# RMSNorm sums from a second, token-major load of x, taken on ScalarE, in a hybrid decoder block

## The chip, the core and the metric

The kernel runs on one core of one Trainium2 chip, alone. The metric is the device time of one execution, in microseconds (us); the time before is the median of three runs, 1137.67 us (1136.68 to 1137.91).

A core has engines that run side by side, each through a queue of its own in order: TensorE (PE; its weight loads are listed apart as PEld), VectorE (DVE), ScalarE (ACT), GpSimd (POOL) and SyncE (SP), which here only issues DMAs. Matmuls write to banks of PSUM, which DVE and ACT read; the other tiles are in SBUF.

## The reference

One decoder block over 1024 tokens of width 1024, in float32:

```python
h = _rmsnorm(x, g_mix_pre)                       # x * rsqrt(mean(x*x, -1) + 1e-6) * g
proj = h @ w_in + b_in
u_pool, q, k, v, gates = split(proj)             # widths 512, 512, 128, 128, 2048
y_pool = multiscale_pool(u_pool, w_pool, pool_scale)
q, k = partial_rotary(q), partial_rotary(k)      # 8 query heads, 2 key/value heads of 64
y_attn = sliding_window_sink_attention(q, k, v)  # blocks of 128 tokens, window 128
g_pool, g_attn = split(sigmoid(gates))
mix = (g_pool * (y_pool @ w_branch_pool) + g_attn * (y_attn @ w_branch_attn)) @ w_out
x = x + _rmsnorm(mix, g_mix_post)
h2 = _rmsnorm(x, g_mlp_pre)
x = x + _rmsnorm(square(relu(h2 @ w_up)) @ w_down, g_mlp_post)
```

The change concerns only the first line, the sum of x*x for each token, and the order of work up to the end of attention.

## The kernel before

Tokens are taken in 8 blocks of 128 (index n), the width in 8 slices of 128 (index k). Each float32 operand is split into a high and a low part (`split`: ACT makes the high part at L101, DVE the low part at L104), and each product is three matmuls, high x high, low x high and high x low (`PASSES`).

**The load stage** (L205 to L242) runs over k. `xt[k]` is x with the width on the partitions and the 1024 tokens along the free axis. Each step loads `xt[k]` (512 KB) and the weights `w_qkv[k]` (384 KB), on SP's queue. ACT writes the high part of x times the norm's gain (L227), DVE the low part (L228), in two halves of 512 tokens; both split the weights. Then PE adds slice k to the queries (`mm_q`, L183) and to the keys and values (`mm_kv`, L192) of blocks 0 to 3, which stay open in PSUM over all k. The row factor r1 of the norm is not needed for this: it is applied later.

For r1, ACT squares `xt[k]` (L233, L235, in place), and POOL (for the last k, DVE) adds the squares up in `sq` (L236). The load of a later step into the same tile waits for that add. The tile tags bound how far loads run ahead: x tiles have 4 buffers (`s4`), staged weights 3 (`st`). The order of instructions in this stage is set by the scheduler of the framework, from the program order and the dependencies.

**The start of attention** (from L722) is ordered by hand for PE, DVE and ACT. `sq` is still a sum with the width on the partitions, so eight products with a column of ones (L725, 16 instructions on PE, `ones` is a column of `vec`) give the token sums in PSUM (`bss`). `rsqrt` turns them into r1 (L109 on ACT, then a chain on DVE). `pre_qkv(n)` scales the queries, keys and values of a block by r1, adds the bias (L264, L265, on DVE, which frees their PSUM banks) and applies the rotary embedding (L272 to L275, on DVE for block 0, on POOL for the others). `post_qkv(n)` transposes queries and keys on PE (L294, L295), splits them (ACT and DVE) and copies the values (POOL). `score` (L333), `softmax_*`, `attend_t` (L376) and `attend_v` (L394) follow.

**The filler.** All other products of this phase come from a generator, `others()`: queries, then keys and values of blocks 4 to 7, then the pooling branch's products. `fill(t)` takes steps from it until t microseconds of an assumed cost are spent (a query step of three matmuls counts 0.681, a key/value step 0.36); what is spent too much is owed by the next `fill`. So `fill` says how much of that work PE does at each place in the order. Its PSUM banks carry the tag `mm` (3 buffers): the queries of blocks 2 and 3 hold two of them until `pre_qkv(2)` and `pre_qkv(3)` have read them. `load_u(g)` stages weights of the pooling branch, and a list `between` holds the split of them until `flush` puts it in the order.

Everything behind attention (gates, output, MLP in seven products of halves) is left as it is.

Of the kernel before, what the change touches and what calls it, by code (L numbers as in the profile page):

```python
# [8 lines left out]
F32 = mybir.dt.float32  # L9
F32R = mybir.dt.float32r  # L10
AF = mybir.ActivationFunctionType
ALU = mybir.AluOpType
AX = mybir.AxisListType

P = 128
S = 1024
D = 1024
NT = S // P
NK = D // P
# [23 lines left out]
V_BU = V_G + 8  # L43
V_BG = V_BU + 4
V_PS = V_BG + 16
V_ONE = V_PS + 4
V_N = V_ONE + 1


@with_exitstack  # L50
def block_kernel(ctx: ExitStack, tc, xt, x, consts, vecs, sinks, b_qkv, g_post, g_mlp, g_mlp_post,
                 w_qkv, w_u, w_g, w_pool, w_bp, w_ba, w_o, w_up, w_dn, x1_dram, spill, wbp_dram, f_dram, out):
    nc = tc.nc
# [30 lines left out]
    def at(tag, bufs, shape, dt=F32):  # L84
        return ap_.tile([P] + shape, dt, tag=tag, name=nm(tag), bufs=bufs)

    def bank(tag, shape=None):
        return psum["pool"].tile([P] + (shape or [512]), F32, tag=tag, name=nm(tag), bufs=psum["bufs"][tag])
# [100 lines left out]
    def mm_kv(n, k, joint=False):  # L189

        for j, (xh, h) in enumerate(PASSES):
            pe.matmul(bkv_of(n), xs_[k][n // 4][:, xh, n % 4 * P:(n % 4 + 1) * P],  # L192
                      wkv[k // 2][:, h, k % 2, :], start=k == 0 and j == 0 and not (joint and n % 2),
                      stop=k == NK - 1 and j == 2 and not (joint and n % 2 == 0))
# [1 line left out]
    bq01 = bank("sc", [2, 512])  # L196
    bq = {0: bq01[:, 0, :], 1: bq01[:, 1, :], 2: bank("mm"), 3: bank("mm")}
    bkv = {0: bank("at", [2, 256]), 2: bank("at", [2, 256])}
    bss = bank("at", [NT])
    bz = bank("mm")  # L200
    for j in range(11):
        pe.matmul(bz, zeros[:, 0, :P], zeros[:, 0, :], start=j == 0, stop=j == 10)
    sq = at("qkv", 3, [S])
    ones = vec[:, V_ONE:V_ONE + 1]
    for k in range(NK):  # L205
        xs = at("s4", 4, [S])
        ws = stage([768]) if k else ws_first
        if k < 2:
            nc.sync.dma_start(xs[:, :512], xt[k][:, :512])
            if k:  # L210
                nc.sync.dma_start(ws, w_qkv[k])
            else:
                nc.sync.dma_start(vec, vecs)
                nc.sync.dma_start(ws[:, 512:], w_qkv[k][:, 512:])
            nc.sync.dma_start(xs[:, 512:], xt[k][:, 512:])
        else:
            nc.sync.dma_start(xs, xt[k])
            nc.sync.dma_start(ws, w_qkv[k])
        halves_ = [xp.tile([P, 2, 512], F32R, tag="x", name=nm("x")) for _ in range(2)]
        gk = vec[:, V_G + k:V_G + k + 1]  # L220
        q = wslot([2, 512]) if k < 6 else ga_.tile([P, 2, 512], F32R, tag="ga", name=nm("wq"))
        if k % 2 == 0:
            wkv.append(ga_.tile([P, 2, 2, 256], F32R, tag="ga", name=nm("wkv")))
        kv = wkv[-1]
        for th, t in enumerate(halves_):
            c = slice(th * 512, (th + 1) * 512)
            act.activation(t[:, 0, :], xs[:, c], AF.Identity, scale=gk)  # L227
            dve.scalar_tensor_tensor(t[:, 1, :], xs[:, c], gk, f32(t[:, 0, :]), ALU.mult, ALU.subtract)  # L228
            if th == 0:
                split(q[:, 0, :], q[:, 1, :], ws[:, :512])  # L230
                split(kv[:, 0, k % 2, :], kv[:, 1, k % 2, :], ws[:, 512:])
        if k == 0:
            act.activation(sq, xs, AF.Square)  # L233
        else:
            act.activation(xs, xs, AF.Square)  # L235
            (pool if k < NK - 1 else dve).tensor_tensor(sq, sq, xs, ALU.add)  # L236
        xs_.append(halves_)
        wq.append(q)
        for n in range(4):
            mm_q(n, k, bq[n])  # L240
        for n in range(4):
            mm_kv(n, k, joint=True)  # L242
    nc.sync.dma_start(cst, consts)
    nc.sync.dma_start(snk, sinks.unsqueeze(0).broadcast_to([P, NH]))
    bq_b = bcast(b_qkv, 768)
# [291 lines left out]
    def flush(todo):  # L537
        while todo:
            todo.pop(0)()
# [66 lines left out]
    def others():  # L606
        for n in range(4, NT):
            flush(late)
            bq[n] = bank("mm")
            for k in range(NK):  # L610
                mm_q(n, k, bq[n])
                yield 3 * 0.227
            if n == NT - 1:
                load_u(3)
                flush(between[1])
            bkv[n] = bank("at" if n == 4 else "mm", [1, 256])
            for k in range(NK):
                mm_kv(n, k)
                yield 3 * 0.12
            if n == 4:  # L620
                late.append(lambda: pre_qkv(4))
            else:
                pre_qkv(n)
        wps = stage([4, P])
        nc.sync.dma_start(wps, w_pool)
        between[0].append(lambda: split(wpt[:, 0], wpt[:, 1], wps))
        wpt = bcp.tile([P, 2, 4, P], F32R, tag="bc", name="wpt")
        wpts.append(wpt)
        for gi in (3, 2, 1, 0):
            load_wb(gi)  # L630
            if gi:
                load_u(gi - 1)
            yield from u_half(gi, 0)
            if gi < 3:
                yield from wb_half(gi + 1, 1)
            yield from u_half(gi, 1)
            yield from wb_half(gi, 0)
        yield from wb_half(0, 1)
# [81 lines left out]

    LOW, HIGH = range(4), range(4, 8)
    with tc.manual_schedule(engines={mybir.EngineType.PE, mybir.EngineType.DVE, mybir.EngineType.Activation}):  # L722
        for n in range(NT):
            fill(0.34)
            pe.matmul(bss[:, n:n + 1], sq[:, n * P:(n + 1) * P], ones, start=n == 0, stop=n == NT - 1)  # L725
        rsqrt(r1, bss[:, :NT], NT)
        act.activation(warm, r1[:, :1], AF.Exp)
        pre_qkv(0)
        pre_qkv(1)
        fill(5.4)  # L730
        post_qkv(0)
        pre_qkv(2)
        fill(2.8)
        score(0, 0)
        score_prev(0, 0)
        pre_qkv(3)
        fill(1.0)
        score(0, 1)
        score_prev(0, 1)
        fill(0.7)  # L740
        post_qkv(1)
        softmax_max(0)
        make_rb(0)
        fill(0.7)
        make_rb(1)
        softmax_exp(0, range(3))
        fill(1.8)
        score(1, 0)
        score_prev(1, 0)
        softmax_exp(0, range(3, 8))  # L750
        post_qkv(2)
        fill(0.7)
        score(1, 1)
        softmax_scale(0)
        score_prev(1, 1)
        softmax_max(1)
        fill(3.7)
        sums = {}

        def pump(k, gi):  # L760

            if gi not in sums:
                sums[gi] = pool_in(gi, us[gi], y_place)
            for _ in range(k):
                next(sums[gi])

        for n in range(NT):
            attend_t(n)
            if n == 0:
                softmax_exp(1, LOW)  # L770
            if n + 2 < NT:
                score(n + 2, 0)
            if n + 1 < NT:
                softmax_exp(n + 1, HIGH)
            if n + 2 < NT:
                score_prev(n + 2, 0)
            attend_own(n)
            if n + 1 < NT:
                softmax_scale(n + 1)
            flush(late)  # L780
            if n in (4, 5):
                pump(1, 3)
            elif n == 6:
                pump(1, 2)
            fill(3.6)
            if n + 2 < NT:
                score(n + 2, 1)
                score_prev(n + 2, 1)
                softmax_max(n + 2)
            if n + 3 < NT:  # L790
                post_qkv(n + 3)
            if n + 2 < NT:
                softmax_exp(n + 2, LOW)
            if n == 4:
                pump(1, 3)
            elif n == 5:
                pump(2, 3)
                nc.sync.dma_start(u_dram[3], us.pop(3))
            elif n == 6:
                pump(2, 2)  # L800
                load_x(0, lambda: at("qkv", 3, [S]))
            elif n == 7:
                pump(1, 2)
                nc.sync.dma_start(u_dram[2], us.pop(2))
                gt.prepare(0)
            fill(3.0 if n == NT - 1 else 4.2)
            attend_v(n)
            if n % 4 == 3:
                for kh in range(2):
                    nc.sync.dma_start(y_dram[n // 4 * 2 + kh], flat(y[n // 4][kh]))  # L810
        gt.prepare(1)
        fill(1e3)
        flush(between[0])
        flush(between[1])
        gt.prepare(2)
        load_x(1, lambda: ga_.tile([P, S], F32, tag="ga", name=nm("xr")))
        for _ in build_gate(0, lambda: xp.tile([P, 2, 512], F32R, tag="x", name=nm("T"))):
            pass
# [565 lines left out]
def _layout(inputs):  # L1384
    a = {k: np.asarray(v) for k, v in inputs.items()}
    f = np.float32
# [16 lines left out]
    for col, t in ((C_COS, np.cos(ang)), (C_SIN, np.sin(ang))):  # L1403
# [4 lines left out]
        b_in[:512].reshape(4, P).T,  # L1408
        b_in[1280:].reshape(16, P).T,
        a["pool_scale"][0].reshape(4, P).T,  # L1410
        np.ones((P, 1), f),
    ], axis=1)
    return [
        ("xt", c(x.T).reshape(NK, P, S)),
# [38 lines left out]
```

## Time and profile before

| | |
|---|---|
| runs | 1136.68, 1137.67, 1137.91 us; median 1137.67 |
| span of the profiled execution, first to last instruction | 1136.2 us |
| median less that span | 1.5 us |
| PE busy | 1120.7 us, 99% of the span |
| DVE, ACT, POOL busy | 822.7, 523.9, 65.3 us |
| mean granted clock of TensorE | 0.996 |
| DMA | 186.94 MB, mean 165 GB/s |

The profile is of one execution. Its own time is the span, with whatever lies before the first and behind the last instruction, which the profile does not show. A busy PE is not PE at its peak: a lower granted clock makes the same matmul longer and still busy.

### The profile page before, as it was taken

The page shows a single profiled execution, that of the slowest core. Times are in us where ns is not written, and L with a number is a line of the kernel's source. Part 1 is how long each engine was busy: PE and PEld are TensorE (multiplying, and loading weights), DVE is VectorE, ACT ScalarE, POOL GpSimd, SP SyncE. Part 2 cuts the span into 40 slices and gives each one's busy share as a digit, 9 for nine tenths or more (in the row PEclk, how much of TensorE's full clock was granted, in tenths as well). Part 3 has the DMA queues.
Part 4 walks back from the last instruction along what each step waited for, and adds up shares of the span by engine and source line. Part 5 has one row for each costly group of instructions (what it writes and reads, how often), then busy time and mean ns, then how long its engine had stood idle before and what let it go on. Part 6 is the DMA issues. An engine that isn't in the chain of part 4 may idle for free.

```text
span 1136.2 us, 14006 instructions
## 1 busy us (share of the span) xinstructions
PE 1120.7 (99%) x5213; PEld 926.6 (82%) x5213; DVE 822.7 (72%) x1210; ACT 523.9 (46%) x912; POOL 65.3 (6%) x110
## 2 busy tenths in 40 slices
PE   8999999999999999999999999999999999999997
PEld 7888888888888888888788888888888888888885
DVE  7668797899956685677998666666457955446887
ACT  6346655454522234455655444444444345344352
POOL 3432100000000230000000000000000000000000
PEclk9999999999999999999999999999999999999999
DMA  7202338356664434333265343434687765332652
GB/s 247 84 1 74 116 108 297 129 188 229 217 234 161 139 142 155 112 145 111 108 236 206 139 164 142 160 146 156 223 321 278 244 198 193 109 93 74 219 191 91
DMA packets 72052, 186.94 MB, mean 165 GB/s; under 512 B 6448, under 2 KB 10672, under 8 KB 71984
## 3 DMA queue, kind: packets, MB, share of 16 engines
q1 hardware_dynamic: 66368, 166.38, 42.0%
q10 hardware_dynamic: 5616, 19.66, 4.5%
q8 instruction: 41, 0.67, 0.2%
q14 instruction: 27, 0.22, 0.1%
HBM read 132.54 MB, written 53.48 MB: 164 GB/s over the span
## 4 chain that ended last, share of the span: by engine, by line
PE 91%; DVE 5%; ACT 2%; DMA 2%; issue 1%; DVEq 0%
PE mm L485 22%; PE at L485 15%; PE at L1291 14%; PE mm L1291 11%; PE mm L1008 6%; PE mm L422 5%; PE mm L575 4%; PE mm L183 3%; PE mm L424 3%; PE at L394 2%; PE sc L333 1%; PE at L1008 1%; PE at L192 1%; DVE wh L104 1%; DMA st<-in_w_up_dram 1%
## 5 line engine op out<-in xcount | busy, mean ns | idle before, releaser
L1291 PE MATMUL at<-ar,wh 128*128 128x512 f32 x744 | 169.6, 389 | 0.0
L1291 PEld LDWEIGHTS at<-ar,wh 128*128 128x128 f32 x744 | 139.6, 188 | 29.3 <-DVE ar L104 0.4
L1291 PE MATMUL mm<-ar,wh 128*128 128x512 f32 x576 | 131.0, 389 | 0.0
L104 DVE TENSOR_TENSOR wh<-raw,wh 128x1024 fp32r<-128x1024 f32 x53 | 64.8, 1223 | 85.4 <-ACT wh L101 85.4
L1291 PEld LDWEIGHTS mm<-ar,wh 128*128 128x128 f32 x576 | 108.1, 188 | 22.5
L101 ACT CAST wh<-raw 128x1024 fp32r<-128x1024 f32 x53 | 55.8, 1053 | 135.8 <-PE at L1291 61.9
L101 ACT CAST wh<-st 128x512 fp32r<-128x512 f32 (+1 forms) x105 | 66.2, 642 | 104.0 <-PE at L485 31.0
L104 DVE TENSOR_TENSOR wh<-st,wh 128x512 fp32r<-128x512 f32 (+1 forms) x105 | 81.8, 790 | 25.9 <-ACT wh L101 23.3
L485 PE MATMUL mm<-gr,wh 128*128 128x512 f32 x309 | 74.5, 390 | 0.1
L485 PEld LDWEIGHTS mm<-gr,wh 128*128 128x128 f32 x309 | 57.7, 188 | 12.3 <-ACT g L1073 0.5
L485 PE MATMUL mm<-T,wx 128*128 128x512 f32 x288 | 67.6, 389 | 0.0
L485 PEld LDWEIGHTS mm<-T,wx 128*128 128x128 f32 x288 | 54.1, 188 | 11.2
L485 PE MATMUL at<-T,wx 128*128 128x512 f32 x252 | 59.1, 389 | 0.0
L485 PEld LDWEIGHTS at<-T,wx 128*128 128x128 f32 x252 | 47.3, 188 | 9.8
L485 PE MATMUL mm<-x,wh 128*128 128x512 f32 x240 | 55.2, 389 | 0.0
L485 PEld LDWEIGHTS mm<-x,wh 128*128 128x128 f32 x240 | 45.0, 188 | 9.4
L104 DVE TENSOR_TENSOR ar<-B,ar 128x1024 fp32r<-128x1024 f32 x37 | 45.1, 1219 | 5.3 <-ACT ar L101 5.0
L575 PE MATMUL mm<-x,wh 128*128 128x512 f32 x192 | 47.5, 396 | 0.0
L485 PE MATMUL at<-gr,wh 128*128 128x512 f32 x174 | 42.4, 390 | 0.0
L101 ACT CAST ar<-B 128x1024 fp32r<-128x1024 f32 x37 | 38.9, 1050 | 7.5 <-DMA B<-in_w_dn_dram 4.7
L575 PEld LDWEIGHTS mm<-x,wh 128*128 128x128 f32 x192 | 35.2, 188 | 7.7
L485 PEld LDWEIGHTS at<-gr,wh 128*128 128x128 f32 x174 | 32.6, 188 | 7.3 <-DVE gr L104 0.5
(368 smaller groups left out, 2182.9 us busy)
## 6 DMA issues: line engine op xcount, KB each, us to landing
raw<-f_dram SPq DMA_DIRECT2D x53, 512.0 KB, 3.7
f_dram<-g SPq DMA_DIRECT2D x30, 512.0 KB, 3.3
B<-in_w_dn_dram SPq DMA_DIRECT2D x24, 512.0 KB, 6.2
st<-in_w_up_dram SPq DMA_DIRECT2D x22, 512.0 KB, 3.5
st<-in_w_g_dram SPq DMA_DIRECT2D x18, 512.0 KB, 3.6
f_dram<-g ACTq DMA_DIRECT2D x17, 512.0 KB, 2.6
g<-spill_dram SPq DMA_DIRECT2D x16, 512.0 KB, 4.5
raw<-in_w_dn_dram SPq DMA_DIRECT2D x16, 512.0 KB, 4.6
```

The lines of the kernel that those rows point to most:

```text
L101: act.copy(hi, src)
L104: eng.tensor_tensor(lo, src, f32(hi), ALU.subtract)
L183: pe.matmul(bq, xs_[k][n // 4][:, xh, n % 4 * P:(n % 4 + 1) * P], wq[k][:, h, :], start=k == 0 and j == 0, stop=k == NK - 1 and j == 2)
L192: pe.matmul(bkv_of(n), xs_[k][n // 4][:, xh, n % 4 * P:(n % 4 + 1) * P], wkv[k // 2][:, h, k % 2, :], start=k == 0 and j == 0 and not (joi ...
L333: pe.matmul(sb[:, kv, i, :nk], qt[r, qx, m * P:(m + 1) * P], kx[r, k0:k0 + nk], start=j == 0, stop=j == 2)
L394: pe.matmul(yb.rearrange("p m q -> p (m q)"), v[:, vh, kv * HD:kv * HD + P], p[ph][:, 4 * kv:4 * kv + 4].rearrange("p i q -> p (i q)"), st ...
L422: pe.matmul(bs[th], whi[:, k, :], rhs(k, hl, th), start=k == 0 and hl == 0, stop=False)
L424: pe.matmul(bs[th], wlo[:, k, :], rhs(k, 0, th), start=False, stop=k == nk - 1)
L485: pe.matmul(b, w[:, wh, kt, :], xo[kt][:, xh, :], start=not after and kt == 0 and j == 0, stop=kt == 3 and j == 2, skip_group_check=after)
L575: pe.matmul(b, (whi, wlo)[h][:, k, :], xr(k, xh, th), start=j == 0, stop=j == len(mms) - 1)
L1008: pe.matmul(obs[n][dj], l, wos[k][whl][:, dj * 512:(dj + 1) * 512], start=k == 0 and hl == 0 and whl == 0, stop=k == NK - 1 and hl == 1)
L1291: pe.matmul(bs[t], fo[fh][:, k2, t * P:(t + 1) * P], wo_[wh][:, k2, :], start=not after and s2 == 0 and k2 == 0 and j == 0, stop=s2 == NS ...
```

## The change

- The eight squares of `xt[k]`, the seven adds and the 16 instructions of L725 go, with `bss`, `sq` and the column of ones.
- x is loaded a second time, with tokens on the partitions: eight loads of `x[n]` (512 KB each), each squared on ACT with the sum over the free axis written to `ssq[:, n]`. The loads of `token_square(n)` take tiles of the tag `s8` (3 buffers), which the scores use later. `token_square(0)` stands in the step k = 2, and so on; 6 and 7 behind the loop.
- `rsqrt` reads `ssq` directly.
- In the order by hand, the eight `fill(0.34)` between the products go, `pre_qkv(2)` stands ahead of `post_qkv(0)`, and `fill(5.4)` becomes `fill(7.0)`.
- In `others()`, `load_u(3)` and the `flush` of `between[1]` come earlier: the load after the queries of block 6, the flush in the middle of those of block 7.

The short description of the change also says that keys of the second half are made ahead of queries; in the diff, `mm_kv(n)` follows `mm_q(n)` in `others()` as before.

```diff
@@ load stage
-    bss = bank("at", [NT])
...
-    sq = at("qkv", 3, [S])
-    ones = vec[:, V_ONE:V_ONE + 1]
+    ssq = sp.tile([P, NT], F32, name="ssq", bufs=1)
+
+    def token_square(n):
+
+        t = at("s8", 3, [D])
+        nc.sync.dma_start(t, x[n])
+        act.activation(t, t, AF.Square, accum_out=ssq[:, n:n + 1])
+
     for k in range(NK):
...
-        if k == 0:
-            act.activation(sq, xs, AF.Square)
-        else:
-            act.activation(xs, xs, AF.Square)
-            (pool if k < NK - 1 else dve).tensor_tensor(sq, sq, xs, ALU.add)
+        if k >= 2:
+            token_square(k - 2)
...
         for n in range(4):
             mm_kv(n, k, joint=True)
+    for n in (6, 7):
+        token_square(n)
     nc.sync.dma_start(cst, consts)
@@ others()
             for k in range(NK):
                 mm_q(n, k, bq[n])
+                if n == NT - 1 and k == 3:
+                    flush(between[1])
                 yield 3 * 0.227
-            if n == NT - 1:
+            if n == NT - 2:
                 load_u(3)
-                flush(between[1])
@@ order by hand
-        for n in range(NT):
-            fill(0.34)
-            pe.matmul(bss[:, n:n + 1], sq[:, n * P:(n + 1) * P], ones, start=n == 0, stop=n == NT - 1)
-        rsqrt(r1, bss[:, :NT], NT)
+        rsqrt(r1, ssq, NT)
         act.activation(warm, r1[:, :1], AF.Exp)
         pre_qkv(0)
         pre_qkv(1)
-        fill(5.4)
+        pre_qkv(2)
+        fill(7.0)
         post_qkv(0)
-        pre_qkv(2)
         fill(2.8)
         score(0, 0)
```

More of the change, by code (lines that the diff above doesn't have):

```diff
@@ L45 @@
 V_PS = V_BG + 16
-V_ONE = V_PS + 4
-V_N = V_ONE + 1
+V_N = V_PS + 4
 @with_exitstack
@@ L1410, in _layout @@
         a["pool_scale"][0].reshape(4, P).T,
-        np.ones((P, 1), f),
     ], axis=1)
```

## The prediction

> **What bounds the kernel now.** I read the page first, for the share of each engine; then the busy time by stretches of time; then the timeline and the chain of waits for the first 62 us, the only part that the change touches.
>
> ```profile
> span 1136.2 us, 14006 instructions
> PE 1120.7 (99%) x5213; PEld 926.6 (82%) x5213; DVE 822.7 (72%) x1210; ACT 523.9 (46%) x912; POOL 65.3 (6%) x110
> ```
>
> TensorE (PE) is busy 99% of the span, so time is gained only where PE idles, runs at a low clock, or does work that can go. All of it ahead of the attention loop is in the stretches below: start:end, length, then busy time and (instructions) of PE, PEld, DVE, ACT and POOL, the granted clock, the DMA share and GB/s.
>
> ```profile
> 0.00:8.00 8.00, 6.38 (x19) 4.52 (x20) 2.88 (x7) 4.34 (x7) 1.25 (x11) 1.00 0.72 212
> 8.00:14.00 6.00, 6.00 (x36) 5.31 (x35) 3.98 (x7) 5.33 (x10) 1.05 (x1) 1.00 1.03 408
> 14.00:24.00 10.00, 8.45 (x46) 6.90 (x45) 9.69 (x8) 7.55 (x13) 6.48 (x3) 1.00 0.54 191
> 24.00:30.00 6.00, 6.00 (x39) 5.42 (x38) 5.84 (x8) 3.11 (x5) 2.41 (x1) 1.00 0.74 239
> 33.45:37.63 4.18, 4.18 (x26) 3.69 (x25) 4.05 (x6) 2.22 (x4) 1.94 (x2) 1.00 0.27 65
> 52.85:55.52 2.67, 0.00 (x0) 0.00 (x0) 1.69 (x4) 0.85 (x2) 2.17 (x7) 1.00 0.00 0
> 55.52:60.12 4.60, 4.60 (x14) 3.37 (x14) 1.39 (x3) 0.00 (x0) 4.10 (x12) 0.63 0.00 0
> ```
>
> One step k of the load stage takes PE 4.18 us when nothing holds it (the fifth row). At 52.85 PE stands still for 2.67 us, and afterwards the clock is granted at 0.63. The chain of waits (start, length, what) shows what PE does from the end of the load stage on:
>
> ```profile
> 40.66 1.43 PE at L192 x12
> 42.09 0.69 PE mm L183 x3
> 42.79 0.34 PE at L725 x4
> 46.21 0.34 PE at L725 x4
> 46.55 2.87 PE mm L183 x12
> 49.42 2.88 PE at L192 x24
> 52.30 0.44 PE sc L294 x4
> 54.81 0.67 DVE y L264
> 55.52 4.60 PE mm L183 x12
> 60.12 0.82 PE sc L333 x12
> ```
>
> **The 16 matmuls.** L725 sums the squares over partitions: 16 instructions, woven into the queries of block 4. From 42.09 to 46.55 stand 12 query matmuls and the 16 of L725, 4.46 us; the next 12 queries alone took 2.87, so the 16 cost at least 1.59. By the step (12 queries and 12 shorter ones in 4.18, the shorter at 2.88 / 24 = 0.12 each) a query is 0.2285 and the 16 cost 4.46 - 2.74 = 1.72. I take **1.7**: pure PE work, it leaves the path whole.
>
> **The stall at 52.85.** The queries of block 5 need a PSUM bank that is freed only by DVE's L264 of `pre_qkv(2)`, the chain's step before 55.52, which stands behind both splits of `post_qkv(0)` on DVE. The change puts `pre_qkv(2)` ahead of `post_qkv(0)`, so the bank is free before PE asks. That takes away 2.67 us of idleness, and the slow clock behind it: 12 queries took 4.60 where 12 x 0.2285 is 2.74, 1.86 more. Together **4.5**.
>
> A rule can be set beside this pair. The Trainium skill's page "TensorE: Matmul & The Clock Gate", Part 1, has the clock halved only after an idle window of about 3.4 us; by that, a 2.67 us wait need not have cost any clock and the term would be 2.7. The trace disagrees (2.67 idle, then 0.63), and the measurement decides.
>
> What is late next? After the load stage PE now does `fill(7.0)`: 8 query steps of 3 x 0.2285 and 5 key/value steps of 3 x 0.12, 5.5 + 1.8 = 7.3 us, and then transposes block 0. By then DVE has to have finished this:
>
> ```profile
> 46.59 0.27 ACT L109 ACTIVATE sm<-at,eps 128x8 f32<-128x8 f32 x1 [4.33 <-PE at L725]
> 47.81 0.17 DVE L121 TENSOR_TENSOR r<-sm,sm 128x8 f32<-128x8 f32 x1
> 48.01 0.75 DVE L264 SCALAR_TENSOR_TENSOR qkv<-sc,r,bc 128x512 f32<-128x512 f32 x1
> 50.19 0.74 DVE L264 SCALAR_TENSOR_TENSOR qkv<-sc,r,bc 128x512 f32<-128x512 f32 x1
> 50.85 0.48 DVE L265 SCALAR_TENSOR_TENSOR qkv<-at,r,bc 128x256 f32<-128x256 f32 x1
> 40.98 1.28 ACT L109 ACT_TABLE_LOAD   x1
> 68.42 0.18 ACT L359 ACTIVATION_READ_ACCUMULATOR s<-s,nmx 128x1 f32 x1
> ```
>
> `pre_qkv(0)` takes 50.19 - 48.01 = 2.2 us, the two after it 51.33 - 50.19 = 1.1 each. If the sums are ready, DVE does the three in 4.4 us from the end of the load stage, 2.9 ahead of PE's transposes. Now behind 1.1 us of `pre_qkv(2)` on DVE, the splits of `post_qkv(0)` wait for those transposes anyway. On POOL its four rotations may go ahead of the value copies of block 0, which only `attend_v(0)` reads:
>
> ```profile
> 87.09 1.53 PE L394 MATMUL at<-s,v 128*128 128x512 f32 x6
> ```
>
> Some 30 us lie between, so that costs nothing. One filler step (0.7 us) fewer is done by the first score; it is done later, which is no gain. Between the two scores of block 0 stands one filler query step of 0.69 instead of two; ScalarE's copy out of their single bank needs about that, so I allow 0.1 us of new waiting.
>
> **The adds.** For the second and third steps PE's weight loads waited for DVE (`wh`, L104):
>
> ```profile
> 14.63 0.19 PEld L183 LDWEIGHTS sc<-wh,x 128*128 128x128 f32 x1
> 19.89 0.19 PEld L183 LDWEIGHTS sc<-wh,x 128*128 128x128 f32 x1
> 25.09 1.24 PEld L183 LDWEIGHTS sc<-wh,x 128*128 128x128 f32 x6
> 29.27 1.24 PEld L183 LDWEIGHTS sc<-wh,x 128*128 128x128 f32 x6
> 9.89 0.69 DVE L104 TENSOR_TENSOR wh<-st,wh 128x512 fp32r<-128x512 f32 x1
> 12.95 2.41 POOL L236 TENSOR_TENSOR qkv<-qkv,s 128x1024 f32<-128x1024 f32 x1 [11.17 <-ACT s L235]
> 13.41 2.49 DVE L104 TENSOR_TENSOR wh<-st,wh 128x512 fp32r<-128x512 f32 x1 [0.70 <-ACT wh L101]
> ```
>
> The weight loads of the third to sixth steps begin at 14.63, 19.89, 25.09 and 29.27: 5.26 and 5.20 apart, then 4.18. The split for the third step started on DVE 0.5 us into a POOL add of 2.41 and took 2.49, against 0.69 for the same split at 9.89, and PE had to wait for it. With the adds gone the two steps return to 4.18: 1.08 + 1.02 = **2.1** us. The later adds also stretch DVE's work but delay no step of PE (the pitch is 4.18 already), so they give nothing more. The last add, on DVE, goes as well, and ScalarE keeps eight squares.
>
> **What is added: eight loads of 512 KB.** They go on SP's queue in program order, one behind each step's pair from the third step on, the last three behind the last pair; `consts`, `sinks` and `b_qkv` come behind them.
>
> ```profile
> s<-in_xt_dram SPq DMA_DIRECT2D x6, 512.0 KB, 5.8
> st<-in_w_qkv_dram SPq DMA_DIRECT2D x7, 384.0 KB, 5.7
> 0.00:41.80 41.80, 38.62 (x202) 32.57 (x203) 32.59 (x37) 27.29 (x43) 16.02 (x17) 1.00 0.66 223
> 4.63 0.62 ACT L101 CAST wh<-st 128x512 fp32r<-128x512 f32 x1 [1.96 <-DMA st<-in_w_qkv_dram]
> 11.82 1.04 ACT L235 ACTIVATE s<-s 128x1024 f32<-128x1024 f32 x1
> ```
>
> A step brings 512 + 384 KB = 0.92 MB, a token load 0.52. By 14 us 8 x 0.212 + 6 x 0.408 = 4.14 MB have moved. The last step's weights stand behind eight steps and five token loads, 9.96 MB, and the last token load ends at 11.53 MB. For the rate I take 408 GB/s, the row in which the queue never ran dry (share 1.03); the lower bound is the 239 of 24 to 30 us, where the share was only 0.74, so that a full queue there would give an estimated 239 / 0.74 = 323. The last weights land at 14 + 5.82 / 0.408 = 28.3 us (32.0 at 323, 38.4 at 239), the last tokens at 32.1 (36.9; 44.9).
>
> PE wants the last step at 42.09 - 2.1 - 4.18 = 35.8, and cast, split and the low half of x before it take 0.62 + 0.69 + about 0.7 = 2.0 us. So the weights may land as late as 33.8: hidden at 408 and 323, not at 239. After the last tokens come the square 1.04, the read of the accumulator 0.18, the table load 1.28, the root 0.27 and DVE's chain to r1 (46.86 to 47.98) 1.1: 3.9 us, r1 at 36 to 41. PE's transposes come at 40.0 + 7.3 = 47.3, and need `pre_qkv(0)` (2.2) and the first operation of `pre_qkv(1)`, which frees their bank (0.75); r1 may come as late as 44.3, the last tokens at 40.4. ScalarE was busy 27.3 of the first 41.8 us and gets 8 x 0.18 more, so it has the room.
>
> The Trainium skill's page "DMA: Bandwidth & Descriptors", section "Where 436 GB/s comes from", speaks against this part: loads from HBM are bound near 358 GB/s per core. By it a step with its token load would take an estimated 1.44 / 0.358 = 4.0 us, just under PE's 4.18, so the sum stays and only the margin shrinks. The trace disagrees with 408 over six microseconds, and that counts.
>
> **Edits with one answer.** `flush(between[1])` moves to the middle of block 7's queries and `load_u(3)` one block ahead. Fewer filler steps are done by then, and with the move both splits fall into the same filler stretch as before, so ScalarE and DVE keep their order: nothing. On SP the loads of `w_u`, `w_pool` and `w_bp` keep their order behind the new ones. The words on keys made ahead of queries have no edit behind them: in `others()` `mm_kv(n)` still follows `mm_q(n)`; this half of the description is worth nothing either way.
>
> **Sum.** 1.7 + 4.5 + 2.1 - 0.1 = 8.2 us off the profiled span of 1136.2, so 1128.0. The median of the runs is 1137.67, 1.47 above that span; I keep this distance: **1129.5**.
>
> **Rivals.** *The load stage gives nothing.* Something else holds DVE or PE there, for instance `nsnk` on DVE, which waits for `sinks`, a load that now stands behind all the token loads, with the last splits queued behind it. For it: it is unknown where `nsnk` will stand on DVE. Against: the long split ended with the POOL add. The gain is 8.2 - 2.1 = 6.1: 1131.6.
>
> *The sums come late*, in place of the old wait. The token tiles have three buffers, so the seventh and eighth load wait for earlier squares, and a turn of load and square takes 5.8 + 1.2 = 7.0 us. One such turn behind the last weights (28.3 to 32.0) ends by 39.0, in time. With two the last tokens land at up to 32.0 + 7.0 + 5.8 = 44.8, 4.4 late; with the slow clock 1.9 more, 6.3 in all, gain 1.9: 1135.8. A turn that half overlaps comes 1 us late: 1130.5. The middle is 1133.
>
> *Slower: the queue starves PE.* SP issues in order, so a token load that waits for its buffer holds the next step's x and weights. If that leaves the rate at the 191 GB/s of 14 to 24 us, when loads waited for buffers too, the last weights land at 14 + 5.82 / 0.191 = 44.5, 10.7 late; minus 8.2 that is 2.5 slower, 4.4 with one slow clock: 1140.2 to 1142.1, say 1141. It turns the sign where the weights land 8.2 late, at 42.0, a rate of 208. For it: 191 and 239 are measured. Against: much of that was SP waiting until POOL's add had read an x tile (total, times, longest), which goes:
>
> ```profile
> SPq L217 <- POOL qkv L236: 7.9, 2, 4.0
> ```
>
>
> **How the numbers follow.** Chances: forecast 0.74, no gain in the load stage 0.08, late sums 0.10, starved 0.08. The measurement can tell about 0.2% (2.3 us) from no change. Faster: 0.74 + 0.08 + 0.06 of the late sums = 0.88. Same: the other 0.04 and 0.01 of the starved case = 0.05. Slower: 0.07. The low end, 1127.8, is the forecast less the 1.0 by which the lowest run before lay under the median and 0.7 for the filler step, if it fills a gap later. The high end, 1133.5, takes in the first rival and half of the second; the other half and the slower case stay outside, 0.13, with little of the forecast.
>
> **What would show it.** Right: no L725 and no L236; weight loads of the third to sixth steps 4.2 apart; end of the load stage near 40.0; no PE gap and clock 1.00 from there to the first score (L333), which starts near 51 instead of 60.12; SP not waiting for an x tile's buffer. Wrong: PE waiting in the load stage for a cast or a DMA; the root (L109) later than 43 with DVE or PE behind it; a new gap of over 2 us with a clock under 1.00; or all these shifts present and the span not 8 us shorter, which would mean that a later stage takes the time back.

## The result and the profile after

The changed kernel takes **1149.26 us** (median of 4 runs, 1149.24 to 1149.97) against 1137.79 before: ratio 1.0103, 95% interval 1.009 to 1.0116. It is 11.5 us slower, where 8.2 us faster was forecast.

The page after, of an execution of 1149.25 us:

```profile
span 1147.5 us, 13978 instructions
PE 1136.7 (99%) x5197; PEld 922.5 (80%) x5197; DVE 808.1 (70%) x1209; ACT 526.6 (46%) x920; POOL 50.6 (4%) x104
```

PE has 16 instructions fewer and is busy 16.0 us longer, at a mean clock of 0.999 against 0.996 before. It does not wait more (the rest of the span is 10.8 us against 15.5): the same work takes longer. Line numbers shift a little with the edit: L183, L192, L333 and L1291 of before are L182, L191, L336 and L1292 after. The start, which the prediction was about, is nevertheless as it was forecast. First the stretches of time after, columns as before:

```profile
8.00:14.00 6.00, 6.00 (x36) 5.21 (x35) 4.59 (x9) 4.90 (x9) 0.00 (x0) 1.00 1.02 411
14.00:24.00 10.00, 10.00 (x61) 8.79 (x60) 6.44 (x12) 9.04 (x17) 0.00 (x0) 1.00 1.03 405
24.00:30.00 6.00, 6.00 (x33) 5.14 (x32) 3.45 (x7) 5.44 (x11) 0.00 (x0) 1.00 1.03 408
52.85:55.52 2.67, 2.67 (x26) 2.32 (x25) 2.38 (x4) 0.90 (x2) 2.67 (x7) 1.00 0.00 0
```

The loads run at 405 to 411 GB/s for 22 us on end and PE is busy all through; the hole at 52.85 is gone, and so is the slow clock. The timeline after, with the steps of the load stage and r1:

```profile
14.71 1.24 PEld L182 LDWEIGHTS sc<-wh,x 128*128 128x128 f32 x6
18.93 1.24 PEld L182 LDWEIGHTS sc<-wh,x 128*128 128x128 f32 x6
23.15 1.24 PEld L182 LDWEIGHTS sc<-wh,x 128*128 128x128 f32 x6
38.01 0.17 DVE L120 TENSOR_TENSOR r<-sm,sm 128x8 f32<-128x8 f32 x1
```

The chain of waits after:

```profile
38.80 1.43 PE at L191 x12
40.23 5.56 PE mm L182 x24
51.30 0.82 PE sc L336 x12
```

The load stage ends at 40.23 (forecast 40.0), r1 is ready at 38.2 (36 to 41), and the first score starts at 51.30 (near 51) instead of 60.12. One thing is off: a step takes 4.22 us, not 4.18.

That small thing is the first sign of what happened to the whole kernel. From here on "product" means one matmul instruction. In the ones below, PEld first loads an operand of 128x128 (the weights), and PE then streams one of 128x512 past it (the moving operand); a `wh` tile can be either. The chain in the last stage, which the diff does not touch, before:

```profile
823.83 43.52 PE at L1291 x192
867.35 43.52 PE mm L1291 x192
```

and after:

```profile
826.39 44.80 PE at L1292 x192
871.19 44.80 PE mm L1292 x192
```

The groups of about the first six such pieces, those that write `at` (count, busy us, mean ns of one, idle before), before:

```profile
L1291 PE MATMUL at<-ar,wh 128*128 128x512 f32 x552 | 125.6, 389 | 0.0
L1291 PEld LDWEIGHTS at<-ar,wh 128*128 128x128 f32 x552 | 103.6, 188 | 21.5
```

and after:

```profile
L1292 PE MATMUL at<-ar,wh 128*128 128x512 f32 x552 | 129.3, 395 | 0.0
L1292 PEld LDWEIGHTS at<-ar,wh 128*128 128x128 f32 x552 | 103.5, 187 | 25.3
```

The same 192 products take 44.80 instead of 43.52 us: 233.3 ns each from start to start instead of 226.7, without any wait, and the weight loads themselves are as fast as before. It is not everywhere. Two groups of the page before:

```profile
L485 PE MATMUL mm<-T,wx 128*128 128x512 f32 x288 | 67.6, 389 | 0.0
L485 PE MATMUL mm<-gr,wh 128*128 128x512 f32 x309 | 74.5, 390 | 0.1
```

and of the page after:

```profile
L488 PE MATMUL mm<-T,wx 128*128 128x512 f32 x288 | 67.7, 389 | 0.0
L488 PE MATMUL mm<-gr,wh 128*128 128x512 f32 x309 | 76.4, 396 | 0.0
```

Products with `wh` are slower, those with `wx` are not. All `wh` tiles come from the pool wp. What follows is read from the built programs, which the profile does not show. The `wh` tiles start at byte 24032 of a partition before and at 24000 after: the column of ones that left `vec` took 32 bytes (in steps of 32) out of the pool cp, and bcp, st and wp moved down. `ssq`, 32 bytes in sp behind wp, put everything further on back where it was. Before, all the large tiles that PE reads started at 480 modulo 512; after, `wh` (and the one weight tile in bcp) at 448 and the others at 480. Of the 4637 products of 512 columns, 3288 then have weights and moving operand 32 bytes apart.

### The profile page after: what moved, and what is told of

It is laid out like the page before. It is cut to its first block, busy times and chain, and to the rows that moved or that the text cites. A ratio compares the mean times of both kernels' runs of the same rounds, so it can differ in the third digit from the quotient of the medians.

```text
span 1147.5 us, 13978 instructions
## 1 busy us (share of the span) xinstructions
PE 1136.7 (99%) x5197; PEld 922.5 (80%) x5197; DVE 808.1 (70%) x1209; ACT 526.6 (46%) x920; POOL 50.6 (4%) x104
## 4 chain that ended last, share of the span: by engine, by line
PE 95%; DVE 3%; DMA 1%; ACT 1%; issue 0%; DVEq 0%
PE mm L488 23%; PE at L488 16%; PE at L1292 16%; PE mm L1292 12%; PE mm L1009 5%; PE mm L425 5%; PE mm L578 4%; PE mm L182 3%; PE mm L427 3%; PE at L397 2%; PE at L191 1%; PE sc L336 1%; PE at L1009 1%; PE sc L182 1%; PE mm L191 1%; DMA st<-in_w_up_dram 1%
## 5 line engine op out<-in xcount | busy, mean ns | idle before, releaser
L1292 PE MATMUL at<-ar,wh 128*128 128x512 f32 x744 | 174.4, 395 | 0.0
L1292 PEld LDWEIGHTS at<-ar,wh 128*128 128x128 f32 x744 | 139.4, 187 | 34.3 <-DVE ar L103 0.3
L1292 PE MATMUL mm<-ar,wh 128*128 128x512 f32 x576 | 134.9, 395 | 0.0
L1292 PEld LDWEIGHTS mm<-ar,wh 128*128 128x128 f32 x576 | 108.0, 187 | 26.4
L103 DVE TENSOR_TENSOR wh<-st,wh 128x512 fp32r<-128x512 f32 (+1 forms) x105 | 78.2, 754 | 26.7 <-ACT wh L100 24.3
L488 PE MATMUL mm<-x,wh 128*128 128x512 f32 x240 | 56.8, 395 | 0.0
L578 PE MATMUL mm<-x,wh 128*128 128x512 f32 x192 | 48.6, 400 | 0.0
```

The lines of the kernel that those rows point to most:

```text
L103: eng.tensor_tensor(lo, src, f32(hi), ALU.subtract)
L488: pe.matmul(b, w[:, wh, kt, :], xo[kt][:, xh, :], start=not after and kt == 0 and j == 0, stop=kt == 3 and j == 2, skip_group_check=after)
L578: pe.matmul(b, (whi, wlo)[h][:, k, :], xr(k, xh, th), start=j == 0, stop=j == len(mms) - 1)
L1292: pe.matmul(bs[t], fo[fh][:, k2, t * P:(t + 1) * P], wo_[wh][:, k2, :], start=not after and s2 == 0 and k2 == 0 and j == 0, stop=s2 == NS ...
```

## The experiments

Theory A: the distance between the two operands' addresses sets the time of a product. Rival B: the second load or the new order makes PE slower, addresses play no part.

**Only the addresses put back.** 

> The changed kernel with one word changed: ssq is taken from the pool cp instead of sp. The column of ones that left vec moved the tiles of bcp, st and wp (the weights wh) down by 32 bytes; ssq in cp moves them back, and all PE operands start at 32 modulo 64 bytes as before the change. Theory A (a product whose weights and moving operand start at different places modulo 64 bytes takes 6 to 7 ns longer, 234 ns from start to start instead of 227): the 512-column products return to 227 ns, the last stage's 192 products to 43.5 us, and the time is the predicted 1129.5 (1128.5 to 1131). Rival B (the second load of x, or the new order, leaves PE slower; addresses play no part): 1149, 234 ns.

```diff
-    ssq = sp.tile([P, NT], F32, name="ssq", bufs=1)
+    ssq = cp.tile([P, NT], F32, name="ssq")
```

Measured: 1129.56 us (1129.23 to 1130.2), ratio to before 0.9931 (0.9917 to 0.9945). One word takes back 19.7 us and gives the forecast time to 0.1 us. B falls.

**Only the addresses moved, in the kernel before.** 

> The kernel before, with its order and its sums, and two dead 32-byte tiles, one in cp and one in sp: wh starts at 0 modulo 64, everything else at 32, the pattern of the changed kernel. Theory A: 3288 products of 512 columns have operands at different places, 6 to 7 ns each: 20 to 22 us slower than before, 1157 to 1160. Rival B: 1137.8.

```diff
+    shift_w = cp.tile([P, NT], F32, name="shift_w")
+    dve.memset(shift_w, 0.0)
+    shift_b = sp.tile([P, NT], F32, name="shift_b", bufs=1)
+    dve.memset(shift_b, 0.0)
     pad = sp.tile([P, 32], F32, name="pad", bufs=1)
```

Measured: 1159.38 us in one run, 21.7 slower, with nothing of the change in it. The layout is not quite the pattern of the changed kernel, though. 3288 products are 32 bytes apart, as there, but ga, ap and what follows moved by 64, so that 495 others are 64 apart. By the table further down these cost an estimated 2.8 us (447 x 6 ns and 48 x 2 ns), which fits with 21.7 here against 19.7 there. So that the time lies inside the expected 1157 to 1160 is partly luck.

**Which alignment?** Three other layouts follow. A1 says that the distance counts, A2 that weights at a multiple of 64 are slow in themselves.

> The changed kernel with dead 32-byte tiles in sp and at the top of the right side, so that all PE operands start at 0 modulo 64. Theory A1 (a mismatch between the two operands costs): all 4637 products of 512 columns match, 227 ns, 1129.5. Theory A2 (weights at 0 modulo 64 are slow in themselves): all 4637 are slow, 30 us over 1129.5, about 1160. Rival B: 1149.

```diff
+    top = ctx.enter_context(tc.tile_pool(name="top", bufs=1, side="right"))
+    shift_t = top.tile([P, NT], F32, name="shift_t")
...
+    shift_b = sp.tile([P, NT], F32, name="shift_b", bufs=1)
```

Measured: 1138.26 us, ratio to before 1.001 (1.0001 to 1.0019). Neither value: the layout was not as uniform as I took it to be, since ga, ap and what follows stood 64 bytes off the rest modulo 512.

> The changed kernel with the 33rd column of vec back (unused): wh at 32 modulo 64, the tiles of the left side behind it (ga, ap, gp) at 0, those of the right side at 32. Theory A1: 2514 products mismatch (2067 with the moving operand at 0 and the weights at 32, 447 the other way), 15 to 17 us over 1129.5, 1145 to 1147, each mismatched pair near 234 ns in both directions. Theory A2: only the 726 with weights at 0 are slow, 4 to 5 us, 1134. Rival B: 1149.

```diff
-V_N = V_PS + 4
+V_N = V_PS + 5
...
         a["pool_scale"][0].reshape(4, P).T,
+        np.ones((P, 1), f),
```

Measured: 1145.73 us, as A1 has it; A2 had 1134.

> The changed kernel with ssq in a 32-byte pool at the top of the right side: every tile that PE reads stands 32 bytes below its place in the kernel before, so all stand at 448 modulo 512 instead of 480, and all distances between operands are those of before. The third run had them all at 0 modulo 64, but its ga and ap tiles 64 bytes off the others (0 against 448 modulo 512). Theory A1 with a coarser grain (only the distance between the two operands counts, in a block larger than 64 bytes): 1129.5. Theory A2 (a start at 0 modulo 64 costs something by itself): 1134 to 1139.

```diff
+    top = ctx.enter_context(tc.tile_pool(name="top", bufs=1, side="right"))
...
-    ssq = sp.tile([P, NT], F32, name="ssq", bufs=1)
+    ssq = top.tile([P, NT], F32, name="ssq")
```

Measured: 1129.76 us, ratio 0.9935 (0.9918 to 0.9951): with all tiles at 448 the kernel is as fast as with all at 480. Of the two, only the distance counts; A2 falls.

**How coarse is it?** The fast version with dead bytes in sp, which move ga, ap and what follows (2514 products):

```diff
+    shift_b = sp.tile([P, 16], F32, name="shift_b", bufs=1)   # 16, 32, 64 columns: 64, 128, 256 bytes
+    dve.memset(shift_b, 0.0)
```

> The fast version of the first run (ssq in cp) with 64 dead bytes in sp: ga, ap and the tiles behind them 64 bytes up, wh and the right side as before; 2514 products get operands 64 bytes apart modulo 512. If the grain is 64 bytes: 1129.5. If it is 128 or more: the excess of the third run, where the same products were 64 apart, 8.7 us: 1138.

> As the run with 64 dead bytes, with 128. Grain of 64 or 128 bytes: 1129.5. Grain of 256 or more: 4 to 9 us more, 1133 to 1138.

> As the run with 64 dead bytes, with 256. Grain of 256 bytes or less: 1129.5. Grain of 512: 2 to 9 us more, 1131 to 1138.

Measured: 1138.13, 1145.63 and 1129.09 us, one run each; the layouts that were run more often spread by about 1 us, far less than these differences. A distance of 128 bytes costs and one of 256 does not, so in these layouts the grain is 256 bytes. The miss is in size: 128 apart costs as much as 32 apart, where I had bounded it by the 64's. One piece of the chain of the last stage in each of these runs. With ssq in cp (the fast version):

```profile
858.86 43.52 PE mm L1292 x192
```

The kernel before, shifted:

```profile
881.34 44.80 PE mm L1295 x192
```

All at 0:

```profile
865.16 43.95 PE mm L1297 x192
```

The others at 0:

```profile
867.60 44.80 PE mm L1292 x192
```

All 32 lower:

```profile
858.59 43.52 PE mm L1293 x192
```

The left side 64 bytes up:

```profile
865.10 43.95 PE mm L1294 x192
```

128 bytes up:

```profile
867.57 44.80 PE mm L1294 x192
```

256 bytes up:

```profile
858.47 43.52 PE mm L1294 x192
```

192 products take one of three times: 43.52 where the operands are 0 or 256 apart, 43.95 at 64, 44.80 at 32 or 128. Over all products of 512 columns, from the start times in the traces and the addresses in the built programs (moving operand minus the weights loaded beside it, modulo 256):

```
distance    0    32    64   128   192   224
median ns  227   234   229   232   233   232 to 234
```

The distance is to the weights of the *next* product. In the changed kernel 41 products with mismatched weights of their own are followed by matching ones; their median is 227. In 35 it is the other way round, and all of these take 235. That speaks for the next weight load and the running product meeting in their reads. It is not shown: it is read off the trace, no run took the weight load away, and at 64 bytes it does not hold as it stands, since in the run with all at 0 the 24 products of which only the next weights are 64 off, up or down, have a median of 226.

**The order alone.** 

> The kernel before with one line moved: pre_qkv(2) stands ahead of post_qkv(0), fill(5.4) between. Addresses, adds, matmuls with ones as before. Theory of the prediction (the wait for the bank of block 2 and the slow clock behind it cost 4.5 us): no PE gap between 52 and 56 us, clock 1.00, 1137.7 - 4.5 = 1133.2. Rival (the gap comes back at the next wait, or the clock falls anyway): 1135.8 to 1137.7.

```diff
         pre_qkv(1)
+        pre_qkv(2)
         fill(5.4)
         post_qkv(0)
-        pre_qkv(2)
```

Measured: 1133.32 us (1132.96 to 1133.51), ratio 0.9965 (0.9952 to 0.9977). The chain of waits of this run:

```profile
52.88 2.75 PE mm L183 x12
55.63 0.81 PE sc L333 x12
```

The 12 queries take 2.75 us instead of 4.60 and follow without a gap; the first score comes 4.49 us earlier.

**The adds alone.** 

> The kernel before without the six adds on POOL (the sum then holds only the first and the last square; the rest of the work is all there). Theory of the prediction (POOL's add holds up DVE's split and so PE's third and fourth step): these splits take 0.7 us, the steps 4.2 instead of 5.2, 1137.7 - 2.1 = 1135.6. Rival (something else paces these steps): 1137.7.

```diff
-            (pool if k < NK - 1 else dve).tensor_tensor(sq, sq, xs, ALU.add)
+            if k == NK - 1:
+                dve.tensor_tensor(sq, sq, xs, ALU.add)
```

Measured: 1135.84 us, ratio 0.9985 (0.9976 to 0.9994), a gain of 1.7. The weight loads of the steps, from the timeline:

```profile
15.01 1.24 PEld L183 LDWEIGHTS sc<-wh,x 128*128 128x128 f32 x6
19.19 1.24 PEld L183 LDWEIGHTS sc<-wh,x 128*128 128x128 f32 x6
23.37 1.24 PEld L183 LDWEIGHTS sc<-wh,x 128*128 128x128 f32 x6
11.05 1.00 PEld L183 LDWEIGHTS sc<-wh,x 128*128 128x128 f32 x5 [0.58 <-DVE wh L104]
```

The DVE splits of `wh` for the third and fourth step, which started beside a POOL add before and took 2.49 and 2.56 us:

```profile
13.63 0.69 DVE L104 TENSOR_TENSOR wh<-st,wh 128x512 fp32r<-128x512 f32 x1 [0.95 <-ACT wh L101]
17.24 0.69 DVE L104 TENSOR_TENSOR wh<-st,wh 128x512 fp32r<-128x512 f32 x1 [0.60 <-ACT wh L101]
```

They take 0.69 again, and the weight loads of the third to fifth step begin 4.18 apart; a new wait of 0.58 us in the second step, where DVE's split came late in this order, takes a part back.

**The flush back.** 

> The fast version (ssq in cp) with load_u(3) and the flush back at their old places. The prediction gives these two edits nothing because they keep the splits in the same filler stretch; without them the two splits come behind the transposes of block 4 on ACT and DVE. Theory: within 0.3 us of 1129.5, since PE reaches u_half(3) some 6 us after them. Rival: a wait of PE at the first product with wu[3], up to 2 us: 1131.5.

```diff
-                if n == NT - 1 and k == 3:
-                    flush(between[1])
...
-            if n == NT - 2:
+            if n == NT - 1:
                 load_u(3)
+                flush(between[1])
```

Measured: 1132.85 us (1131.74 to 1133.77) against 1129.56 with the edit: 3.3 slower, over both expectations. The timeline of PE and ACT:

```profile
91.50 2.01 PE L578 MATMUL mm<-x,wh 128*128 128x512 f32 x4 [2.27 <-ACT wh L100]
90.42 1.03 ACT L100 CAST wh<-st 128x1024 fp32r<-128x1024 f32 x1
```

The stretch behind it, columns as before:

```profile
91.50:95.00 3.50, 3.50 (x8) 2.75 (x9) 2.26 (x3) 0.00 (x0) 0.00 (x0) 0.51 0.34 91
```

ACT makes the high part of `wu[3]` only behind the copies and exponentials of the next block, PE waits 2.27 us for it, and some 3.4 us follow at half the clock (by finer windows, from about 91.6 to 95.0).

## Why the prediction was wrong

**The step that failed** is the list "Edits with one answer" and the inventory ahead of it. They went through what each removed and added line *does*, and never through where it *lies*. The column of ones and `ssq` are 32 bytes each, in pools on either side of wp; the prediction names neither as a term. What stood in that place is 19.7 us: 3288 products at 6.0 ns each. So the sum held for a kernel with the old layout (1129.56 against 1129.5) and not for this one. The range took in only waits and rates of the first 62 us, and no rival was about the other thousand. Its last sign of being wrong did name this case, all the shifts present and the span not 8 us shorter because a later stage takes the time back; that is what came, without a cause or a chance for it. With the old layout the terms read from the traces (4.49, 1.95 and 1.7, below) add up to the 8.1 us that were gained. By the runs alone the first two are 0.3 and 0.4 under the forecast, within their intervals, so the agreement to 0.1 us is closer than these runs can tell; that much of it is luck.

**The slower rival** had the sign but not the cause: nothing starved. The loads kept 405 GB/s and more, as forecast from the row with a full queue, and the 191 had indeed been for the most part the wait for POOL's add: in the run without the adds alone the row of 14 to 24 us has 313 GB/s. The 239 of 24 to 30 us became only 257 there. The bound of 358 GB/s that the Trainium skill gives ("DMA: Bandwidth & Descriptors", "Where 436 GB/s comes from") does not agree with 405 to 411 over 22 us.

**The stall, 4.5 us:** right. The order alone gives 4.2 by the medians, 4.49 in the trace.

**The adds, 2.1:** mechanism right, a little less in size: 1.7 alone, with the new wait of 0.58 in it. In the fast version the stage ends at 40.14 instead of 42.09, 1.95 earlier.

**The 16 matmuls, 1.7:** not run alone. In the fast version the 24 queries behind the load stage take 5.47 us, 2.74 for 12, so that the 4.46 of before again leaves 1.7. What the two runs leave of the 8.1 us is 8.1 - 4.2 - 1.7 = 2.2, with intervals of two to three microseconds each.

**The flush, nothing:** right for the reason given, since the move keeps the splits in their filler stretch; but the prediction did not price the cover. Without the move the shorter filler at the start would have cost 3.3 us later.

**Late sums:** did not come. r1 was ready at 38.2, with 6 us to spare.

## What to carry to other kernels

Read the diff for bytes as well as for instructions: a tile that is added, removed or resized moves every tile allocated behind it in its pools, and a stage that the diff never touches can change speed. When a group of matmuls with the same shape, clock and no waits has another mean duration, compare tile addresses first; here weights and moving operands had to start at the same place modulo 256 bytes. A short filler stretch that is taken away at one place has to be followed to the next operation that lived under its cover.

## What was not expected of the hardware

- The time from one product of 512 columns to the next depends on the distance between the moving operand and the weights loaded beside it, modulo 256: 227 ns at 0 or 256 bytes, 229 at 64, 232 to 234 at the other distances tried. Why it depends on it, and why 64 in one direction costs a third of the others, is open, and so are distances that are no multiple of 32.
- The clock fell to half after a PE gap of only 2.27 us in the last run (0.51 over the stretch shown), behind 5 us of unbroken work, and after one of 2.67 before the change (0.63 over its stretch). Both are shorter than the idle window of about 3.4 us in the Trainium skill's page "TensorE: Matmul & The Clock Gate", Part 1; the low stretch lasts about 3.4 us in both (91.6 to 95.0, and 56.1 to 59.5), which is as long as the busy window has to be by that page.
